# Two transformer blocks on one core: the third mixer's low parts on VectorE, its units summed in one PSUM bank, its factors folded

## The chip, the core and the metric

The kernel runs on one core of a Trainium2 chip. The metric is the device time of one execution in microseconds. All names of engines are those of the profile: TensorE (PE, and PEld for its weight loads), VectorE (DVE), ScalarE (ACT), GpSimd (POOL) and SyncE (SP), whose queue issues nearly all transfers.

## What is computed

One sequence of 256 tokens with 1024 features passes a first block (a norm, a mixer of pooling, mLSTM and attention, a feed-forward part) and then a second block of two layers. Each layer is feed-forward, mixer, feed-forward, with a layer norm behind each. The mixer of the first layer is a sparse attention (the second mixer of the kernel), that of the second layer is HGRN2, the third mixer, which the change is about:

```python
h = (x @ w_in).astype(F32)                      # 1024 x 4096
zq, zf, zi, zg = jnp.split(h, 4, axis=-1)       # 8 heads of 128 each
q = jax.nn.silu(zq)
log_f = jnp.logaddexp(jnp.log(lbf), jnp.log1p(-lbf) + jax.nn.log_sigmoid(zf))
k = (1.0 - lbf) * jax.nn.sigmoid(-zf)
# per head: S_t = f_t * S_(t-1) + k_t v_t,  o_t = q_t S_t   (v = zi)
o = o * lax.rsqrt(jnp.mean(o * o, axis=-1, keepdims=True) + RMS_EPS) * norm_gain
o = o * jax.nn.silu(zg)
return o.reshape(B, T, D_MODEL) @ w_out
```

`lbf` are bounds per feature, made by a softmax over the layers from a small input; `norm_gain` has one value for each of a head's 128 features. Inputs and output are float32.

## The kernel before, in words

**Products.** All large products are made from two parts of each operand: a high part (a copy to fp32r, on ScalarE, line 265 for weights) and a low part (the value minus the high part, line 268, on VectorE or on GpSimd). A product is hi x hi + hi x lo + lo x hi. Weights come in units of 1 MB, split in two halves of 128 x 1024 each; `get()` hands out the next half, loads units three ahead and splits five halves ahead. A half in the set `pool_halves` has its low part made by GpSimd; `on_pool(len(units) - 14)` puts there 28 halves of the third mixer's input weights, all but those of its first two units.

**Tokens and features.** Activations lie transposed in `XT`, eight chunks of 128 features, high and low part side by side. `gA` makes a unit with features on the partitions: of each half, a whole PSUM bank receives hi x (hi, lo) as one product of 512 columns and lo x hi as one of 256, eight times, so that two halves of the bank have to be added. `evA` does that, per half unit: ScalarE copies one half out (line 428, tile `evs`) and VectorE adds (line 429, tile `z`). `gB` makes a unit with tokens on the partitions, in two banks, one for each 128 tokens, by products of 256 columns. The banks of both come from a pool of two (`psa`).

**The third mixer** (`hgrn_mix`). It begins with the bounds `lb` and `om` = 1 - `lb`: eight small VectorE operations and one exponential (lines 1270 to 1283), and a load of the gain to all partitions. `bulk(u)` makes the four units of the heads 2u and 2u+1: zf, from which two sigmoids give `ff` and `kk` (lines 1312 and 1313), scaled by `om` and `lb` on VectorE (1316 and 1317); zq, which gives `qq` = sigmoid(zq) x zq (1320 and 1321); and the gate and the values (`gv`), with the gate multiplied by the gain on GpSimd (1302). `heads(u)` is the recurrence of two heads in seven levels: in each, TensorE multiplies `kk` with `qe` (lines 1353 and 1356), and VectorE then updates `qe` (1359), `kk` (1360) and `tot` (1362) in place and copies the products to `AT` (1370, or 1368 on ScalarE). After the levels come the products with the values, a norm whose power -1/2 is GpSimd's (516 and 518), and the turn into `MT` by TensorE transposes (`to_XT`, line 500), with a split behind them (487 and 490).

**Order.** `bulk(0)` runs alone; then `drive` lets one step of `bulk(u + 1)` (a half unit) alternate with one step of `heads(u)`, for u = 0, 1, 2, here called stages one, two and three. The last two heads run beside the first products of the output weights (`Out.early`), whose halves are split on VectorE. Instructions keep the order of their engine's queue at run time; where a step is traced is not fixed to the order of the code alone, since a scheduler places instructions by priority.

The first mixer's mLSTM (`mlstm`) makes its weights by eight exponentials at line 801 and multiplies them by products at line 812. `all_vecs` loads small vectors in SP's queue at the kernel's start, ahead of the third load of weights.

Of the kernel before, what the change touches and what calls it, by code (L numbers as in the profile page):

```python
# [9 lines left out]
F32 = mybir.dt.float32  # L10
F32R = mybir.dt.float32r
U32 = mybir.dt.uint32
AF = mybir.ActivationFunctionType
# [4 lines left out]
P = 128  # L18
# [18 lines left out]
# ---------------------------------------------------------------- constants of the shapes  # L37
# [17 lines left out]
def _make_constants():  # L55
# [20 lines left out]
    # rows 0-31: the bucket of the distance 255 - j; row 32: its mask  # L76
# [18 lines left out]
# ---------------------------------------------------------------- kernel  # L95
# [9 lines left out]
def _kern(ctx, tc, nc, A, out):  # L105
# [11 lines left out]
    # ---- x first, then the constants  # L117
    def new_x(rms=False):
        """a tile of tokens; rms: its last element makes the sum of the squares / D the mean of the squares + 1e-6"""
        t = xp.tile([P, D + 1], F32, tag="x", bufs=3, name=nm("x"))  # L120
        if rms:
            POOL.memset(t[:, D : D + 1], 32.0 * 1e-6 ** 0.5)
        return t
# [19 lines left out]
    def queue_behind(i, other):  # L143
        """i after the other in the order of their engine"""
# [3 lines left out]
    # ------------------------------------------------------------ weights  # L148
# [46 lines left out]
    for li in range(2):  # L195
# [14 lines left out]
        else:  # L210
# [4 lines left out]
            on_pool(len(units) - 14)  # L215
# [4 lines left out]
    PF = 3  # units loaded ahead  # L220
    ahead = [5]  # halves split ahead
    barrier = []  # VectorE's instruction that the next low parts wait for
    nxt = [0]  # the next half
    hold = [None, 0]  # the pool and the number of the halves that a feed-forward part holds to its end
# [63 lines left out]
    # ------------------------------------------------------------ small operands  # L288
# [19 lines left out]
    def all_vecs():  # L308
# [6 lines left out]
                ("lb", A["hgrn_lb_2"].rearrange("i (c p) -> (i c) p", p=P)),  # L315
            ]
# [9 lines left out]
    # ------------------------------------------------------------ matmul helpers  # L326
# [12 lines left out]
    later = []  # what is issued behind bulk products of so many ns, and the ns left  # L339

    def behind(ns, ins):
        """issues these, which are last in a chain of other engines, behind the bulk products that run beside that chain"""
        later.append([ns, ins])

    @contextmanager
    def after_bulk(ns):
        """TensorE's part of what is traced here"""
# [18 lines left out]
    def run(g):  # L366
        """the whole of a generator, and what it returns"""
# [6 lines left out]
    def drive(bulk, chains, n):  # L374
        """a step of bulk, then n steps of the chains, until bulk is done"""
# [10 lines left out]
    def gA(XT, alloc=None):  # L386
        """out[c, tok] of one unit of 256 columns, two banks [tt, (hi x hi, with a low part), 128]"""
# [10 lines left out]

    def mmA(XT, alloc=None):
        return run(gA(XT, alloc))  # L400

    def mmB_first(XT):
        """out[tok, c] of two units, the first 128 tokens before the others"""
# [31 lines left out]
    def gB(XT):  # L435
        """out[tok, c] of one unit: two banks, one of each 128 tokens"""
# [14 lines left out]
    def mmN(XT, n, pool, tag, bufs=1):  # L451
        """out[tok, (tt, c)] of a narrow unit of n columns"""
# [16 lines left out]
    def mmD(acc, H, k, w, tts, first, last, hfs=(0, 1)):  # L469
        """acc[tt][hf] += H[:, k] x one row chunk"""  # L470
# [21 lines left out]
    def split_T(XT, k, z):  # L492
        """both parts of z [P, 256 tokens] to chunk k"""
        split_to(XT[:, k, :, 0, :], XT[:, k, :, 1, :], z.rearrange("p (t c) -> p t c", t=2))

    def to_XT(XT, tt, x, k0=0, nk=8, ns=0):
        for q in range(0, nk, 4):
# [6 lines left out]
            split_to(XT[:, ks, tt, 0, :], XT[:, ks, tt, 1, :], ps[:, : w * P].rearrange("p (a b) -> p a b", a=w))  # L504
# [3 lines left out]
    # the table of the first functions  # L508
    ACT.activation(cp.tile([P, 1], F32, name="warm"), mhalf[:, 0:1], AF.Square)

    def rsqrt(src, n, eps):
        """(src + eps) ** -0.5, [P, n]; src in SBUF"""
# [29 lines left out]
    def ln_tile(tt, x, acc, gb, XT, final=False, ns=0):  # L542
# [6 lines left out]
        # mean / 32 and the mean  # L549
        V.tensor_scalar(st[:, 2:3], st[:, 0:1], st[:, 1:2], 1.0 / (32 * D), ALU.add, ALU.mult)  # L550
        # the last element makes the sum of the squares the variance + 1e-5
# [25 lines left out]
    # ------------------------------------------------------------ feed-forward  # L577
    def ffn(XT, conv, half, finish):
        with tc.tile_pool(name=nm("ff"), bufs=2) as fp:
# [17 lines left out]
            def turn(src):  # L597
                """[tok, tt, c] to a bank [c, tok]"""
# [964 lines left out]
```

## Time and profile before

| | us |
|---|---|
| time, median of 3 runs | 1442.87 |
| time, lowest and highest | 1440.56, 1442.90 |
| profiled execution, span from the first to the last instruction | 1438.1 |
| TensorE busy in that span | 1379.6 (96%) |
| VectorE busy | 992.7 (69%) |
| ScalarE busy | 735.8 (51%) |
| GpSimd busy | 189.1 (13%) |

Of the profiled execution the profile gives the span; its own time outside the span is not recorded, and the median stands 4.8 us above it. Matmuls are pipelined, so that a busy TensorE may still run at half its clock: the granted clock (PEclk, 1.00 is 2.4 GHz and 0.50 is 1.2 GHz) has to be read beside the busy time.

In rows that begin with two times and a colon, one stretch of the span is shown: its length, then busy time and number of instructions of TensorE, its weight loads, VectorE, ScalarE and GpSimd, the granted clock, the share of the DMA engines and GB/s. A row of one engine alone has that engine's busy time only. A timeline row has start and length in us, engine, line, operation, output and inputs, shapes and count, and in brackets the idle time before it and what ended it. A row of grouped instructions has, behind the bar, busy time in us and the mean ns of one, then the idle time before them and its releasers.

### The profile page before, as it was taken

Reading aid. Unit: us, or ns where it says so; the run is one execution under the profiler, and the core shown is the slowest. Engines: PE = TensorE matmul, PEld = TensorE weight load, DVE = VectorE, ACT = ScalarE, POOL = GpSimd, SP = SyncE. Lnnn points to the kernel's source line nnn. Section 1 sums busy time; section 2 is a strip of 40 time slices with the busy share of each in tenths; the row PEclk is TensorE's granted clock in tenths of the full one; section 3 lists DMA queues with packets and bytes.
Section 4 is the critical chain, followed back from the end, with each engine's and each line's share of the span. In section 5 each row is a group of like instructions: output and inputs, shape, how many; then the busy total and the mean of one; then the engine's idle time right before and its main releaser. Section 6 shows DMA issues by size and latency. Waiting matters only on the chain.

```text
span 1438.1 us, 20557 instructions
## 1 busy us (share of the span) xinstructions
PE 1379.6 (96%) x7993; PEld 1194.2 (83%) x7993; DVE 992.7 (69%) x1647; ACT 735.8 (51%) x1227; POOL 189.1 (13%) x127
## 2 busy tenths in 40 slices
PE   7899999999999999899999999999997999999997
PEld 6787888888888888688888888888886888788886
DVE  5865799986566766686765576566756777865574
ACT  5555554544554645576554463555643433654561
POOL 1220132120000005300000000000036560100000
PEclk9999999999999999799999999999998999999999
DMA  8433766555565766321665573555744333466560
GB/s 256 153 118 117 235 220 209 187 176 175 181 199 177 243 179 181 111 94 49 216 201 178 195 260 131 192 188 185 247 133 147 108 100 116 148 203 198 182 205 30
DMA packets 185567, 245.37 MB, mean 171 GB/s; under 512 B 7423, under 2 KB 164903, under 8 KB 185469
## 3 DMA queue, kind: packets, MB, share of 16 engines
q1 hardware_dynamic: 184653, 240.80, 51.4%
q0 software_dynamic: 816, 3.25, 0.7%
q8 instruction: 63, 1.03, 0.3%
q14 instruction: 35, 0.29, 0.1%
HBM read 242.95 MB, written 4.23 MB: 172 GB/s over the span
## 4 chain that ended last, share of the span: by engine, by line
PE 52%; DVE 4%; ACT 1%; POOL 1%; issue 1%; DVEq 0%; POOLq 0%; ACTq 0%
PE psa L355 21%; PE acc L355 14%; PE psb L355 12%; PE psb L1216 1%; PE psb L500 1%; PE lev L1356 1%; DVE kk L1360 1%; PE psb L1218 0%; DVE qe L1359 0%; PE psT L1199 0%; DVE ff L1316 0%; POOL rsr L518 0%; PE psS L1170 0%; DVE kk L1317 0%; PE lev L1353 0%
## 5 line engine op out<-in xcount | busy, mean ns | idle before, releaser
L265 ACT ACTIVATE hi<-raw 128x1024 fp32r<-128x1024 f32 x428 | 448.4, 1055 | 344.0 <-PE psa L355 148.4
L268 DVE TENSOR_TENSOR lo<-raw,hi 128x1024 fp32r<-128x1024 f32 x370 | 457.4, 1241 | 240.7 <-ACT hi L265 239.6
L355 PE MATMUL psa<-XT,hi 128*128 128x512 f32 x1136 | 413.4, 402 | 8.2 <-DVE z L429 8.1
L355 PE MATMUL psa<-XT,lo 128*128 128x256 f32 x1136 | 323.3, 285 | 0.0
L355 PE MATMUL psb<-XT,hi 128*128 128x512 f32 x800 | 282.3, 393 | 0.9 <-DVE z L429 0.9
L355 PE MATMUL acc<-hi,H 128*128 128x512 f32 x880 | 281.8, 393 | 0.0
L355 PEld LDWEIGHTS psa<-XT,hi 128*128 128x128 f32 x1136 | 216.7, 191 | 59.4 <-DVE z L429 9.3
L355 PE MATMUL psb<-XT,lo 128*128 128x256 f32 x800 | 223.6, 280 | 0.0
L355 PEld LDWEIGHTS psa<-XT,lo 128*128 128x128 f32 x1136 | 216.9, 191 | 3.6 <-issue 1.5
L355 PE MATMUL psa<-hi,XT 128*128 128x256 f32 (+1 forms) x928 | 200.4, 306 | 1.6 <-ACT XT L487 0.8
L268 POOL TENSOR_TENSOR lo<-raw,hi 128x1024 fp32r<-128x1024 f32 x58 | 148.1, 2566 | 398.0 <-ACT hi L265 360.4
L355 PEld LDWEIGHTS acc<-hi,H 128*128 128x128 f32 x880 | 166.0, 189 | 35.2 <-DVE H L490 0.3
L355 PEld LDWEIGHTS psb<-XT,hi 128*128 128x128 f32 x800 | 150.0, 187 | 36.7 <-DVE z L429 1.3
L355 PE MATMUL acc<-lo,H 128*128 128x512 f32 x440 | 173.7, 395 | 3.9 <-DVE lo L268 3.9
L355 PEld LDWEIGHTS psa<-hi,XT 128*128 128x128 f32 x928 | 153.0, 195 | 7.4 <-ACT XT L487 2.1
L355 PEld LDWEIGHTS psb<-XT,lo 128*128 128x128 f32 x800 | 150.1, 188 | 0.0
L355 PE MATMUL psa<-lo,XT 128*128 128x256 f32 (+1 forms) x464 | 131.7, 301 | 0.2 <-DVE lo L268 0.2
L355 PEld LDWEIGHTS acc<-lo,H 128*128 128x128 f32 x440 | 83.2, 189 | 21.3 <-DVE lo L268 4.8
L355 PEld LDWEIGHTS psa<-lo,XT 128*128 128x128 f32 x464 | 90.2, 194 | 2.4 <-DVE lo L268 0.5
L518 POOL TENSOR_TENSOR rsr<-var,mhalf 128x1 f32<-128x1 f32 x12 | 7.8, 647 | 626.9 <-ACT jk L556 626.9
L429 DVE TENSOR_TENSOR z<-psa,evs 128x256 f32<-128x256 f32 x132 | 55.1, 419 | 23.7 <-ACT evs L428 23.6
L428 ACT ACTIVATE evs<-psa 128x256 f32<-128x256 f32 x134 | 49.3, 368 | 19.2 <-PE psa L355 19.2
(351 smaller groups left out, 1335.3 us busy)
## 6 DMA issues: line engine op xcount, KB each, us to landing
raw<-in_ffn_w_gate_dram SPq DMA_DIRECT2D x44, 1024.0 KB, 5.1
raw<-in_ffn_w_up_dram SPq DMA_DIRECT2D x44, 1024.0 KB, 5.2
raw<-in_ffn_w_down_dram SPq DMA_DIRECT2D x44, 1024.0 KB, 5.0
raw<-in_w_up_dram SPq DMA_DIRECT2D x22, 1024.0 KB, 5.1
raw<-in_hgrn_w_in_dram SPq DMA_DIRECT2D x16, 1024.0 KB, 5.4
raw<-in_w_down_dram SPq DMA_DIRECT2D x11, 1024.0 KB, 4.8
raw<-in_nsa_w_in_dram SPq DMA_DIRECT2D x10, 1024.0 KB, 6.6
raw<-in_w_in_dram SPq DMA_DIRECT2D x9, 1024.0 KB, 6.5
```

What stands on the lines that cost most here:

```text
L265: h = ACT.activation(hi, src, AF.Copy)
L268: i = (POOL if j in pool_halves else V).tensor_tensor(lo, src, hi.bitcast(F32), ALU.subtract)
L355: i = PE.matmul(o, l, r, start=start, stop=stop)
L428: ACT.activation(s, p4[:, :, 1, :], AF.Copy)
L429: V.tensor_tensor(zc, p4[:, :, 0, :], s, ALU.add)
L500: ts = [PE.transpose(ps[:, j * P : (j + 1) * P], x[:, (q + j) * P : (q + j + 1) * P], ident) for j in range(w)]
L518: POOL.tensor_tensor(r[:, :n], src, mhalf[:, :n], ALU.pow)
L1216: PE.matmul(po5[:, 1, j % 2, br], T1[:, 2 * br + sb], vv[br][:, sb, vs], start=(sb == 0), stop=(sb == 1))
L1356: PE.matmul(pl[:, o : o + 64], kk[:, c, tt * P : (tt + 1) * P], q5[:, c, tt * nb : (tt + 1) * nb, 1, :], start=True, stop=True)
L1360: V.tensor_tensor(k5[:, :, :, 0, :], k5[:, :, :, 0, :], t4[:, :, :, 1, None].broadcast_to([P, 2, 2 * nb, m]), ALU.mult)
```

## The change

- The third mixer's 28 halves are no longer put in `pool_halves`; their low parts are made by VectorE.
- `gZ` takes the place of `gA` and `evA` for zf and zq: three products of 256 columns per chunk, all summed in one place, both half units in one bank. The sigmoids and the multiplication with zq read that bank.
- `kk` is no longer multiplied by `om`; `qq` is. `ff` is scaled on ScalarE. The gain is applied in `to_XT`, per partition, in the copy and in the split behind the transposes, and comes in with the small vectors.
- The bounds are made in the first mixer, on tiles that are kept, behind the exponentials of line 801.

Comments are left out in the changed file as well; those lines are not shown.

```diff
             for j in range(4):
                 for part in (1, 0, 3, 2) if j else (3, 2, 1, 0):
                     a_units(W, 1024 * part + 256 * j, 1, "A" if part < 2 else "B")
-            on_pool(len(units) - 14)
             b_units(A["hgrn_w_out_2"], [0, 1, 2, 3])
...
                 ("lb", A["hgrn_lb_2"].rearrange("i (c p) -> (i c) p", p=P)),
+                ("hg", A["hgrn_norm_gain_2"]),
...
+    def gZ(XT, alloc=None):
+        ps = (alloc or psa)()
+        for c in range(2):
+            hi, lo = get()
+            o = ps[:, 256 * c : 256 * c + 256].rearrange("p (t c) -> p t c", t=2)
+            for k in range(8):
+                bulk_mm(o, lo[:, k, :], XT[:, k, :, 0, :], k == 0, False)
+                bulk_mm(o, hi[:, k, :], XT[:, k, :, 0, :], False, False)
+                bulk_mm(o, hi[:, k, :], XT[:, k, :, 1, :], False, k == 7)
+            yield
+        return ps.rearrange("p (c t) -> p c t", c=2)
...
-    def to_XT(XT, tt, x, k0=0, nk=8, ns=0):
+    def to_XT(XT, tt, x, k0=0, nk=8, ns=0, gain=None):
...
-            split_to(XT[:, ks, tt, 0, :], XT[:, ks, tt, 1, :], ps[:, : w * P].rearrange("p (a b) -> p a b", a=w))
+            src = ps[:, : w * P].rearrange("p (a b) -> p a b", a=w)
+            if gain is None:
+                split_to(XT[:, ks, tt, 0, :], XT[:, ks, tt, 1, :], src)
+            else:
+                ACT.activation(XT[:, ks, tt, 0, :], src, AF.Copy, scale=gain)
+                V.scalar_tensor_tensor(XT[:, ks, tt, 1, :], src, gain, XT[:, ks, tt, 0, :].bitcast(F32), ALU.mult, ALU.subtract)
...
-                        ACT.activation(DT[:, h, tt, :], DT[:, h, tt, :], AF.Exp, bias=ee[:, tt, h : h + 1])
+                        i = ACT.activation(DT[:, h, tt, :], DT[:, h, tt, :], AF.Exp, bias=ee[:, tt, h : h + 1])
+                lower_bounds(mp, i)
...
+    bounds = [cp.tile([P, 8], F32, name=n) for n in ("lb", "om")]
+
+    def lower_bounds(mp, behind_):
...
+        V.tensor_tensor(lm, lbv[:, 0], lbv[:, 1], ALU.max)
+        V.tensor_tensor(e, lbv, lm[:, None, :].broadcast_to([P, 2, 8]), ALU.subtract)
+        queue_behind(ACT.activation(e, e, AF.Exp).ins, behind_)
+        V.tensor_tensor(lm, e[:, 0], e[:, 1], ALU.add)
...
-            hg = row_bc(A["hgrn_norm_gain_2"], 128, "hg", pool=mp)
+            lb, om = bounds
...
-                g3 = gz.rearrange("p t c d -> p (t c) d")
-                POOL.tensor_tensor(g3, g3, hg[:, None, :].broadcast_to([P, 4, P]), ALU.mult)
...
-                zf = evA(mp, (yield from gA(XT)), tag="zf", bufs=1)
+                zf = yield from gZ(XT)
...
                     h = 2 * u + c
-                    V.tensor_scalar(ff[:, c], ff[:, c], om[:, h : h + 1], lb[:, h : h + 1], ALU.mult, ALU.add)
-                    V.tensor_scalar(kk[:, c], kk[:, c], om[:, h : h + 1], None, ALU.mult)
-                zq = evA(mp, (yield from gA(XT)), tag="zq", bufs=1)
+                    ACT.activation(ff[:, c], ff[:, c], AF.Identity, scale=om[:, h : h + 1], bias=lb[:, h : h + 1])
+                zq = yield from gZ(XT)
...
                 ACT.activation(qq, zq, AF.Sigmoid)
-                V.tensor_tensor(qq, qq, zq, ALU.mult)
+                for c in range(2):
+                    h = 2 * u + c
+                    V.scalar_tensor_tensor(qq[:, c], qq[:, c], om[:, h : h + 1], zq[:, c], ALU.mult, ALU.mult)
...
-                    to_XT(MT, tt, oo[:, tt], 2 * u, 2, ns=HNS[tt] if u < 3 else 0)
+                    to_XT(MT, tt, oo[:, tt], 2 * u, 2, ns=HNS[tt] if u < 3 else 0, gain=vecs["hg"])
```

## Rows read from the trace of the kernel before

**Rows 1.** Busy time by stretch of the third mixer: two in the hole, three stages.
```profile
1088.30:1095.90 7.60, 0.03 (x2) 0.01 (x1) 7.57 (x7) 1.33 (x2) 6.40 (x3) 0.71 0.68 218
1095.90:1102.20 6.30, 6.30 (x21) 5.39 (x22) 2.49 (x8) 1.57 (x2) 0.00 (x0) 0.54 0.53 165
1102.20:1139.30 37.10, 33.83 (x250) 31.04 (x250) 28.28 (x41) 15.10 (x32) 22.93 (x13) 0.95 0.31 96
1139.30:1177.30 38.00, 34.72 (x254) 31.62 (x254) 29.46 (x45) 15.84 (x34) 22.98 (x14) 0.96 0.35 112
1177.30:1208.10 30.80, 29.83 (x233) 27.25 (x233) 24.62 (x48) 13.41 (x25) 6.41 (x4) 1.00 0.36 124
```

**Rows 2.** Timeline, 1077 to 1112 us: the first hole and an evacuation before it.
```profile
1080.86 0.36 ACT L428 ACTIVATE evs<-psa 128x256 f32<-128x256 f32 x1
...
1082.87 11.83 POOL L268 TENSOR_TENSOR lo<-raw,hi 128x1024 fp32r<-128x1024 f32 x5
...
1085.19 4.96 DVE L1316 TENSOR_SCALAR ff<-ff,om,lb 128x256 f32<-128x256 f32 x2 [0.70 <-ACT ff L1312]
...
1095.89 0.80 PE L355 MATMUL psa<-XT,hi 128*128 128x512 f32 x1 [7.57 <-DVE z L429]
```

**Rows 3.** VectorE's groups by shape in stage three, 1185.8 to 1213 us.
```profile
L268 DVE TENSOR_TENSOR lo<-raw,hi 128x1024 fp32r<-128x1024 f32 x6 | 7.4, 1226 | 2.0 <-ACT hi L265 2.0
...
L1359 DVE TENSOR_TENSOR qe<-qe,tot 128x256 f32<-128x256 f32 x6 | 2.5, 421 | 0.9 <-PE lev L1356 0.9
...
L429 DVE TENSOR_TENSOR z<-psa,evs 128x256 f32<-128x256 f32 x3 | 1.3, 424 | 0.0
...
L1316 DVE TENSOR_SCALAR ff<-ff,om,lb 128x256 f32<-128x256 f32 x2 | 0.7, 413 | 0.7 <-ACT ff L1312 0.7
```

**Rows 4.** Timeline, the holes of stage one (two rows) and of stage two.
```profile
1115.12 2.56 DVE L1359 TENSOR_TENSOR qe<-qe,tot 128x256 f32<-128x256 f32 x1
...
1118.16 0.63 PE L1356 MATMUL lev<-qe,kk 128*128 128x64 f32 x4 [2.69 <-DVE kk L1360]
...
1156.20 0.94 PE L1356 MATMUL lev<-qe,kk 128*128 128x64 f32 x4 [2.68 <-DVE kk L1360]
```

**Rows 5.** TensorE and its clock by stretch, behind the hole of stage one.
```profile
1118.20:1122.30 4.10, 4.10 (x21) 0.58 0.82 256
```

**Rows 6.** GpSimd's low parts of the mixer: shortest, median, longest ns.
```profile
L268 POOL TENSOR_TENSOR lo<-raw,hi x28: 2382/2412/2672, 1045.7 to 1182.4; 128x1024 fp32r<-128x1024 f32 x28
```

**Rows 7.** Busy time by stretch, the second half of stage three.
```profile
1191.00:1208.10 17.10, 17.10 (x152) 16.26 (x152) 14.21 (x29) 7.25 (x13) 1.28 (x1) 1.00 0.36 124
```

**Rows 8.** The chain that ended last: products of a feed-forward unit, and of values.
```profile
1007.49 5.64 PE psa L355 x32
...
1194.68 2.91 PE psa L355 x24
```

**Rows 9.** Groups by shape, 1040 to 1195 us: readers of PSUM, and GpSimd's powers.
```profile
L428 ACT ACTIVATE evs<-psa 128x256 f32<-128x256 f32 x17 | 6.2, 367 | 0.0
...
L518 POOL TENSOR_TENSOR rsr<-rsv,mhalf 128x2 f32<-128x2 f32 x4 | 2.9, 716 | 0.3
...
L1299 DVE TENSOR_TENSOR gz<-gz,psa 128x256 f32<-128x256 f32 x6 | 2.5, 414 | 4.6 <-ACT gz L1298 4.6
...
L487 ACT ACTIVATE XT<-psb 128x512 fp32r<-128x512 f32 x4 | 2.4, 598 | 6.1 <-PE psb L500 6.1
```

**Rows 10.** Timeline, the bounds at the mixer's start and TensorE's wait there.
```profile
1065.32 1.28 ACT L1274 ACT_TABLE_LOAD   x1 [3.08 <-DVE r L552]
...
1067.91 0.17 DVE L1282 TENSOR_SCALAR om<-lb 128x8 f32<-128x8 f32 x1
...
1069.52 0.63 PE L500 MATMUL psb<-ident,x 128*128 128x128 f32 x4 [0.50 <-DVE x L563]
```

**Rows 11.** Timeline of SP's queue: the last small vector, the third weight load.
```profile
10.60 0.32 SPq L297 DMA_DIRECT2D vst<-in_hgrn_lb_dram  x1
11.91 0.40 SPq L239 DMA_DIRECT2D raw<-in_w_in_dram  x1
```

More of the change, by code (lines that the diff above doesn't have):

```diff
@@ L1263, in nsa_mix @@
                     end(g)
+    bounds = [cp.tile([P, 8], F32, name=n) for n in ("lb", "om")]
+    def lower_bounds(mp, behind_):
+        lbv = vecs["lb"].rearrange("p (i h) -> p i h", i=2)
+        lb, om = bounds
+        lm = mp.tile([P, 8], F32, name="lm")
+        e = mp.tile([P, 2, 8], F32, name="lbe")
+        V.tensor_tensor(lm, lbv[:, 0], lbv[:, 1], ALU.max)
+        V.tensor_tensor(e, lbv, lm[:, None, :].broadcast_to([P, 2, 8]), ALU.subtract)
+        queue_behind(ACT.activation(e, e, AF.Exp).ins, behind_)
+        V.tensor_tensor(lm, e[:, 0], e[:, 1], ALU.add)
+        V.reciprocal(lm, lm)
+        V.tensor_tensor(e, e, lm[:, None, :].broadcast_to([P, 2, 8]), ALU.mult)
+        V.tensor_tensor(lb, e[:, 0], e[:, 1], ALU.add)
+        V.tensor_tensor(lb, lb, e[:, 0], ALU.subtract)
+        V.tensor_scalar(om, lb, -1.0, 1.0, ALU.mult, ALU.add)
     def hgrn_mix(XT, MT, W):
@@ L1268, in hgrn_mix @@
             load_consts(4, mp)
-            lbv = vecs["lb"].rearrange("p (i h) -> p i h", i=2)
-            lm = mp.tile([P, 8], F32, name="lm")
-            e = mp.tile([P, 2, 8], F32, name="lbe")
-            V.tensor_tensor(lm, lbv[:, 0], lbv[:, 1], ALU.max)
-            V.tensor_tensor(e, lbv, lm[:, None, :].broadcast_to([P, 2, 8]), ALU.subtract)
-            ACT.activation(e, e, AF.Exp)
-            V.tensor_tensor(lm, e[:, 0], e[:, 1], ALU.add)
-            V.reciprocal(lm, lm)
-            V.tensor_tensor(e, e, lm[:, None, :].broadcast_to([P, 2, 8]), ALU.mult)
-            lb = mp.tile([P, 8], F32, name="lb")
-            V.tensor_tensor(lb, e[:, 0], e[:, 1], ALU.add)
-            V.tensor_tensor(lb, lb, e[:, 0], ALU.subtract)
-            om = mp.tile([P, 8], F32, name="om")
-            V.tensor_scalar(om, lb, -1.0, 1.0, ALU.mult, ALU.add)
-            hg = row_bc(A["hgrn_norm_gain_2"], 128, "hg", pool=mp)
+            lb, om = bounds
             ATs = []
```

## The prediction

> **What bounds the kernel now.** I read the page's slices first: TensorE's row is full almost everywhere, so time can only come out of its few weak slices, and two of those lie where GpSimd's row is highest, in the third mixer. I then cut that mixer into stretches [rows 1]: a first hole at 1088 us, then three stages, in each of which the level chain of two heads runs beside the products of the next two. TensorE is busy 33.83 of 37.1 us in stage one and 34.72 of 38.0 in stage two, but 29.83 of 30.8 in stage three, in which GpSimd has 6.41 us left to do against 22.9. The granted clock has a mean of 0.71 and 0.54 in the two stretches from 1088.3 to 1102.2.
>
> The timeline of the first hole [rows 2] gives the reason. GpSimd subtracts low parts without a pause (11.83 us for five). Beside it two VectorE scalings of ff take 4.96 us; with GpSimd quiet one takes 413 ns [rows 3]. Two scalings of kk wait in the same way, and behind them in VectorE's queue stands the addition z (L429), which frees a PSUM bank: TensorE waits 7.57 us for it. In stage one a multiplication qe takes 2.56 us beside GpSimd [rows 4] (421 ns otherwise [rows 3]), and the products of the next level wait 2.69 us; stage two repeats this with 2.68 us. After each hole TensorE runs for a while at the lower of its two levels, 1.2 GHz: 4.1 us with a mean of 0.58 in stage one [rows 5]. Stage two has the same pattern (mean clock of the whole stage 0.96, stage one 0.95 [rows 1]).
>
> **The change part by part.** *Low parts move from GpSimd to VectorE.* 28 subtractions of 2.41 us leave GpSimd [rows 6]; one takes 1.226 us on VectorE [rows 3], 34.3 us more there in all, about 8 in each of stages one and two, the rest before and in the first stage. What leaves the path: the hole of 7.6 us, and 6.3 us at 0.54, worth 6.3 x 0.46 = 2.9: 10.5 us. Stage one: 2.7 us of waiting and 4.1 x 0.42 = 1.7 of clock: 4.4 us. Stage two the same, 4.4 us. Together 19.3 us.
>
> What is late next is VectorE's own load. Stage three is a model of it, since its splits (of the output weights) already run there: VectorE is busy 24.62 of 30.8 us [rows 1], and TensorE had no idle time in its last 17.1 us [rows 7], and 1.0 us in the whole. For a changed stage I take 24.62, minus four z of 0.42 and four scalings of about 0.41 [rows 3], plus two more splits (2.45): 23.8 us of some 32. That leaves a quarter of the stage free, so I charge stages one and two 0.7 us each, somewhat under stage three's idle time: 1.4 us. Bounds: 0, and the present hole come back, 4.4 us per stage.
>
> *Units summed in one bank.* Each of 16 half units was 8 products of 512 columns and 8 of 256; it becomes 24 of 256, the same columns. Two half units (32 products) of the first form take 5.64 us in the chain, so 2.82 each; 24 products of 256 columns of another unit take 2.91 [rows 8]. That costs 16 x 0.09 = 1.4 us, all on the path. The 16 evacuations on ScalarE (0.37 us) and 16 additions z on VectorE (0.42) vanish; they lay beside other work, apart from the hole counted above.
>
> A bank now holds a whole unit until its last reader is done. For zf these are two sigmoids on ScalarE, with the whole next unit as cover. For zq they are a sigmoid and two multiplications on VectorE: the nearest rows that read PSUM are 0.60 and 0.41 us [rows 9], so about 0.60 + 2 x 0.41 + 0.2 for two hand-overs = 1.6 us after the last product; before it was one evacuation and one addition, 0.8. Three times (heads 2 to 7) this bank is wanted after 12 products of the next unit, half of 2.91, and mostly the products of a level besides. With a high part ahead on ScalarE and a split ahead on VectorE, at 1.23 us for either, the hold is 4.1 us, 2.6 more than the 12 products. I take 0.4 us each, 1.2 in all, nearer to the case without a queue (0.15 each), since both engines are free for much of the stage; bounds 0 and 3 x 2.6 = 7.8. Below nothing it can come out as well: the path from zf to the sigmoids is shorter by 0.8 us, three times, 2.4 us.
>
> Now ScalarE empties the first half's bank at 1080.86 us [rows 2], while the second half is summed in another. The Trainium skill (PSUM — Partial Sum Buffer, PSUM bank collisions raise a hardware error) says that two engines have to be kept apart by bank, not by address. By it no reader of the first half starts before the unit's last product; if it could, this term would be 0.4 us in all and the sum 0.8 lower. No run here shows which.
>
> *Factors folded.* kk's scaling goes into qq, as a factor of its multiplication with zq. ff's goes to ScalarE: 8 instructions there against 16 evacuations removed. The gain leaves GpSimd for the splits behind the transposes, which keep their number: a scaled copy on ScalarE, and on VectorE a form with one operand more. I take 0; the cover is the quarter of the stage in which VectorE is free, and without it I would put 0.1 us on each of 16, 1.6 us.
>
> *Bounds.* A table load (1.28 us) and an exponential leave ScalarE from their place ahead of a layer norm's square, and eight VectorE operations of some 0.17 us go with them [rows 10]. The square then begins 1.3 us earlier; the transposes at the end of its chain found TensorE idle for 0.50 us. Gain 0.5, not more, since before that hole TensorE has other products. In the first mixer the same work comes behind the last exponential of the mLSTM weights (L801), with the table already loaded. There VectorE's sum of the exponentials waits for ScalarE, and behind it would stand the product at L812, which the mLSTM's values need; TensorE has bulk products meanwhile. I take 0.5 us; bounds: 0, and 8 x 0.17 plus a wait as long as a high part and the exponential, some 3 us. A small transfer more in SP's queue puts the third weight load later by at most 1.3 us [rows 11]; the products of the first two units hide that, and without them it costs as much.
>
> **Sum.** Gains 19.3 + 0.5 = 19.8; costs 1.4 + 1.4 + 1.2 + 0.5 = 4.5. Net 15.3 us against the profiled span of 1438.1: 1422.8. The median of the times, 1442.87, lies 4.8 us above that span; with the same distance the forecast is 1427.6.
>
> **The rivals.** *A smaller gain: new holes.* VectorE serves level chain, splits and banks in order; where these meet, TensorE idles long enough to lose its clock. Price: the 4.4 us of stage one in each of three stages, 13.2 us in place of the 2.6 charged for load and banks: 1438. For it: qq's two readings hold a whole bank. Against it: 17.1 us without idle time beside splits on VectorE [rows 7].
>
> *Slower: splits wait at the head of VectorE's queue.* A split needs its high part from ScalarE; issued too early it stops VectorE. The six of stage three waited 2.0 us together [rows 3]; if each waited as long as that, 8 add 16 us per stage to 23.8 us of work and to the 8.8 us that VectorE stands now (37.1 - 28.28 [rows 1]): 48.6 us, 11 more than the present 37.6, in each of two stages. Against that stand 11 us gained in the first hole and the bounds: 11 us slower, 1454. It decides once VectorE's waits in a stage pass 37.6 + 5.5 - 23.8 = 19 us. Against it: 8.8 us now, and 2.0 for six splits.
>
> *The rest of GpSimd still blocks.* Eight powers for rsqrt stay there, 0.72 us each [rows 9], and a split beside one would stop as qe does now [rows 4]: 5.8 us if felt each time, 1433. The Trainium skill (SBUF — State Buffer, Who interferes with whom) has it that VectorE with two SBUF inputs and GpSimd reading SBUF shut each other out for a whole instruction; the trace agrees, with 2.56 us against 0.42. Against the price: VectorE mostly waits for just these powers.
>
> *It does not do what it says:* the holes have a cause other than GpSimd, and only the costs are left: 1447. Against it: the same scaling takes six times as long beside GpSimd as without it.
>
> **How the numbers follow.** Forecast 1427.6, chance 0.69, its own range 1422 (load, bank and first mixer at nothing, zf's 2.4 us gained) to 1432. New holes 0.13, GpSimd's rest 0.10, slower 0.05, another cause 0.03. The range for 8 in 10 reaches from 1420 to 1437. A measurement of this kernel tells 0.2% (2.9 us) from no change. Faster by more: 0.69 + 0.10 + 0.10 = 0.89; slower 0.05 + 0.02 = 0.07; within it the rest, 0.04.
>
> **What would show it.** After: no hole near 1088 us, the clock at 1.00 through the mixer, stages of 31 to 33 us, VectorE's two-input operations at 0.42 us throughout, half units at 2.9. Wrong would be: TensorE idle above 1 us for qq or for a low part, VectorE standing for high parts, a longer mLSTM part in the first mixer.

## The result, and the profile after

The changed kernel takes 1420.87 us (median of 4 runs, 1419.54 to 1423.34), the kernel before 1442.88 beside it (4 runs, 1440.56 to 1444.89): a ratio of 0.9852, with a 95% interval of 0.9838 to 0.9866. That is 22.0 us, where 15.3 were forecast; the time lies inside the range and 6.7 us under the forecast. The profiled span went from 1438.1 to 1417.7 us, 20.4 less, so 5.1 us of the 6.7 are in the span. The other 1.6 us lie in the distance of the median from the profiled span, 4.8 us before and 3.2 now; the forecast had carried the 4.8 over. The changed kernel's profiled execution took 1419.54 us, 1.8 us above its own span, so the rest of the 3.2 is only that this execution was faster than the median.

The page shows it at a glance, in 40 equal slices of the span, each digit a share in tenths. First TensorE and GpSimd in the kernel before, then TensorE, GpSimd and the clock in the changed one:

```profile
PE   7899999999999999899999999999997999999997
...
POOL 1220132120000005300000000000036560100000
```

```profile
PE   7899999998999999799999999999999999999997
...
POOL 1320221220000003500000000000000000100000
PEclk9999999999999999899999999999999999999999
```

The third mixer lies in slices 31 to 35 of the changed kernel. TensorE's row has only nines there, and GpSimd's only zeros up to a 1 in the last; before, the 31st slice of TensorE was a 7. TensorE's two weak slices behind the start are now the 10th and the 17th; the latter, where GpSimd's row has its 5 and the clock its only 8, comes back below.

Busy time by stretch, the changed kernel: the stretch from the mixer's start to the first level, then stages one, two and three (columns as in rows 1):

```profile
1063.60:1090.30 26.70, 26.70 (x227) 26.70 (x226) 18.10 (x31) 15.57 (x22) 1.53 (x3) 1.00 0.50 164
1090.30:1122.10 31.80, 31.80 (x281) 31.02 (x280) 21.16 (x41) 14.64 (x28) 0.27 (x2) 1.00 0.46 143
1122.10:1155.60 33.50, 32.90 (x287) 31.71 (x286) 22.62 (x46) 15.89 (x32) 1.93 (x5) 1.00 0.38 127
1155.60:1186.40 30.80, 30.21 (x261) 28.97 (x260) 22.27 (x45) 14.35 (x25) 1.54 (x3) 1.00 0.37 129
```

Against [rows 1] stage one went from 37.1 to 31.8 us, stage two from 38.0 to 33.5, stage three stayed at 30.8. The stretch ahead of them took 38.0 before (1064.18 to 1102.18) and takes 26.7 (1063.64 to 1090.31). The granted clock is 1.00 throughout, where it was 0.71 and 0.54 in the hole and 0.95 and 0.96 in the stages. That is where the time went: 11.3 + 5.3 + 4.5 = 21.1 us, all inside the third mixer. Its whole length, from the last product ahead of it to the transposes of its last output tile, went from 170.7 to 149.7.

What TensorE waited for from 1060 to 1215 us, the changed kernel (engine, line, waited for: us in total, times, longest):

```profile
PE psb L513 <- DVE oo L1419: 1.9, 7, 0.3
```

This is the whole list. Before, from 1060 to 1240 us, 8.3 us for z and 6.0 us for kk stood in it:

```profile
PE psa L355 <- DVE z L429: 8.3, 2, 7.6
PE lev L1356 <- DVE kk L1360: 6.0, 5, 2.7
```

And VectorE's groups in stage one (1090.3 to 1122.1 us), to be held against [rows 3, 4]:

```profile
L267 DVE TENSOR_TENSOR lo<-raw,hi 128x1024 fp32r<-128x1024 f32 x8 | 9.8, 1226 | 4.2 <-ACT hi L264 4.2
...
L1382 DVE TENSOR_TENSOR qe<-qe,tot 128x256 f32<-128x256 f32 x6 | 2.5, 422 | 1.8 <-PE lev L1379 1.8
L1383 DVE TENSOR_TENSOR kk<-kk,tot 128x256 f32<-128x256 f32 x6 | 2.5, 418 | 0.0
...
L1344 DVE SCALAR_TENSOR_TENSOR qq<-qq,om,psa 128x256 f32<-128x256 f32 x2 | 0.9, 472 | 0.0
```

qe takes 422 ns in the mean instead of up to 2.56 us, and the eight splits of the stage cost VectorE 1226 ns each, with 4.2 us of standing for high parts in all.

### The profile page after: what moved, and what is told of

It reads as the page before. It is cut to its first block, busy times and chain, and to the rows that moved or that the text cites. A ratio compares the mean times of both kernels' runs of the same rounds, so it can differ in the third digit from the quotient of the medians.

```text
span 1417.7 us, 20750 instructions
## 1 busy us (share of the span) xinstructions
PE 1373.5 (97%) x8121; PEld 1194.8 (84%) x8121; DVE 971.8 (69%) x1647; ACT 734.9 (52%) x1218; POOL 116.6 (8%) x95
## 4 chain that ended last, share of the span: by engine, by line
PE 50%; issue 6%; DVE 1%; ACT 1%; POOL 1%; DVEq 0%; POOLq 0%; ACTq 0%
PE psa L355 19%; PE acc L355 13%; PE psb L355 12%; PE psb L1235 1%; PE psb L513 1%; PE psb L1237 0%; POOL rsr L536 0%; PE psT L1218 0%; PE psS L1189 0%; PE lev L1379 0%; PE psT L1220 0%; PE psb L1180 0%; PE psS L1147 0%; PE psS L1191 0%; ACT hi L264 0%
## 5 line engine op out<-in xcount | busy, mean ns | idle before, releaser
L267 DVE TENSOR_TENSOR lo<-raw,hi 128x1024 fp32r<-128x1024 f32 x398 | 492.5, 1243 | 252.2 <-ACT hi L264 251.1
L355 PE MATMUL psa<-XT,hi 128*128 128x512 f32 (+1 forms) x1264 | 410.9, 375 | 3.2 <-DVE z L442 3.0
L355 PEld LDWEIGHTS psa<-XT,hi 128*128 128x128 f32 x1264 | 230.3, 189 | 48.5 <-DVE z L442 4.2
L355 PE MATMUL psa<-hi,XT 128*128 128x256 f32 (+1 forms) x928 | 197.4, 302 | 0.4 <-ACT XT L500 0.3
L355 PEld LDWEIGHTS psa<-hi,XT 128*128 128x128 f32 x928 | 150.8, 192 | 6.2 <-ACT XT L500 1.9
L267 POOL TENSOR_TENSOR lo<-raw,hi 128x1024 fp32r<-128x1024 f32 x30 | 81.1, 2715 | 192.1 <-ACT hi L264 167.4
L442 DVE TENSOR_TENSOR z<-psa,evs 128x256 f32<-128x256 f32 x116 | 48.3, 418 | 16.2 <-ACT evs L441 15.9
L500 ACT ACTIVATE H<-sg 128x512 fp32r<-128x512 f32 x51 | 31.7, 622 | 48.4 <-DVE sg L626 33.8
```

What stands on the lines that cost most here:

```text
L267: i = (POOL if j in pool_halves else V).tensor_tensor(lo, src, hi.bitcast(F32), ALU.subtract)
L355: i = PE.matmul(o, l, r, start=start, stop=stop)
L442: V.tensor_tensor(zc, p4[:, :, 0, :], s, ALU.add)
L500: i = ACT.activation(hi, src, AF.Copy)
```

## The experiments

The theory (A): GpSimd's subtractions stretch VectorE's operations, and their departure from the third mixer is the gain; folding, one bank and bounds only move some us. The rival (B): the shorter chain on VectorE, with its z additions and scalings gone, is a good part of the gain by itself. Each ratio below is to the kernel before, run beside that experiment, with a 95% interval; the length of the mixer is that of one profiled execution.

**The one line alone.** The kernel before, without its subtractions on GpSimd in the third mixer; the rest of the change is left out.

```diff
-            on_pool(len(units) - 14)
             b_units(A["hgrn_w_out_2"], [0, 1, 2, 3])
```

> The kernel before with one line taken out: the 28 low parts of the third mixer are made by VectorE; units are still summed in two halves, factors and bounds stay where they were. Theory A (GpSimd's subtractions are the cause of the holes, the rest is worth nothing): nearly the whole gain, 1421 to 1425 us. Theory B (the holes need both, GpSimd's work and the operations that the folding takes away): VectorE carries more here than in the changed kernel, so new holes, 1430 us or more.

Measured: 1423.41 us (1420.73 to 1424.55), ratio 0.9875 (0.9858 to 0.9892). The mixer is 150.8 us long. One deleted line gives nearly the whole gain: 19.9 of the mixer's 21.0 us, and by the two ratios 18 of 21 us. What TensorE still waited for, 1060 to 1218 us:

```profile
PE lev L1355 <- DVE kk L1359: 1.9, 2, 0.9
PE psb L499 <- DVE oo L1395: 0.7, 3, 0.3
PE psa L354 <- DVE z L428: 0.7, 1, 0.7
PE psb L499 <- DVE x L562: 0.5, 1, 0.5
```

The list still names z and kk, as before the change, but for 2.6 us in place of 14.3. The last line is the layer norm's wait at the mixer's start, which stood there before the change as well [rows 10].

**All but the one line.** The changed kernel, with the subtractions back on GpSimd in that mixer.

```diff
+            on_pool(len(units) - 14)
             b_units(A["hgrn_w_out_2"], [0, 1, 2, 3])
```

> The changed kernel with that one line put back: GpSimd makes the 28 low parts, all else as changed. Theory A: GpSimd still blocks VectorE's operations with two SBUF inputs, and the loss is nearly whole, 1437 to 1442 us. Theory B (two ways to cure the first hole, each enough): the scalings and the additions behind which TensorE stood in the first hole are gone, so only the holes of stages one and two return, 4.4 us each, 1429 to 1432 us.

Measured: 1442.5 us (10 runs, 1436.75 to 1445.21), ratio 1.0003 (0.9989 to 1.0017); the mixer is 168.9 us long. B falls: with GpSimd subtracting, the folded form is worth nothing that the times tell, and 1.8 us by the length of the mixer. TensorE's three longest waits, 1060 to 1230 us, below them two of VectorE's groups from 1080 to 1180, and two rows of VectorE's timeline in the hole:

```profile
PE psS L1360 <- DVE qq L1345: 5.3, 1, 5.3
PE lev L1380 <- DVE kk L1384: 4.5, 4, 1.3
PE lev L1377 <- DVE kk L1384: 3.3, 2, 1.7
```

```profile
L1384 DVE TENSOR_TENSOR kk<-kk,tot 128x256 f32<-128x256 f32 x12 | 13.7, 1142 | 0.0
...
L1345 DVE SCALAR_TENSOR_TENSOR qq<-qq,om,psa 128x256 f32<-128x256 f32 x6 | 2.6, 471 | 0.0
```

```profile
1087.23 9.66 DVE L1386 TENSOR_TENSOR tot<-tot 128x128 f32<-128x128 f32 x6
1096.81 0.86 DVE L1345 SCALAR_TENSOR_TENSOR qq<-qq,om,psa 128x256 f32<-128x256 f32 x2
```

The hole is there although z is gone: it now waits for qq. And qq itself takes 471 ns, no more than in the changed kernel (472). What holds it up stands ahead of it in VectorE's queue: seven small products of the factors (tot), on two operands in SBUF, which took 1.64 us (the first) and 9.66 us (the other six) here. Operations on two SBUF operands are stretched (kk 1142 ns in the mean against 418); the one that reads one operand from SBUF and one from PSUM is not. Two operands are not the whole rule, though: in the first hole of the kernel before, the stretched ones were scalings of ff, with a single tensor in SBUF beside their factors (2.48 us each [rows 2]); with the line deleted the same eight scalings take 412 ns in the mean.

**Reading or presence?** Two kernels keep VectorE's splits as in the change and give GpSimd other work beside them. In the first, GpSimd subtracts a high part from itself, into a tile that nothing uses, at each split of the mixer: work added for this run alone, which reads SBUF as the old subtractions did. In the second, GpSimd only writes: a memset of 128 x 2048, also unused, triggered by a one-column copy on ScalarE.

```diff
+        if j in beside and spare:
+            f = hi.rearrange("p a b -> p (a b)").bitcast(F32)
+            POOL.tensor_tensor(spare[0], f, f, ALU.subtract)
```

> The changed kernel, in which GpSimd makes a subtraction of the same size beside each split of those 28 halves that falls into the mixer (it reads the high part twice and writes a tile that nobody uses); VectorE still makes the low parts, so nothing waits for GpSimd but the buffer of the high part. Theory A (the port between them, not the result's lateness, is what costs): VectorE's two-input operations take up to 2.5 us again, holes and lower clock return, 8 to 25 us slower than the changed kernel. Rival (what cost was that the low parts came late): within 3 us of the changed kernel.

Measured: 1456.72 us (1452.37 to 1457.95), ratio 1.0101 (1.0078 to 1.0125); the mixer is 183.5 us long, 33.8 more than without the reads. That is beyond the 8 to 25 us expected: VectorE now makes its own low parts beside these reads, and they are stretched as well, to 1571 ns in the mean from 1226. TensorE's four longest waits, 1060 to 1240 us, and two of VectorE's groups from 1080 to 1200:

```profile
PE psS L1364 <- DVE qq L1349: 8.3, 1, 8.3
PE lev L1404 <- DVE kk L1388: 6.5, 2, 3.2
PE lev L1384 <- DVE kk L1388: 5.7, 4, 1.8
PE lev L1381 <- DVE kk L1388: 4.1, 4, 1.9
```

```profile
L268 DVE TENSOR_TENSOR lo<-raw,hi 128x1024 fp32r<-128x1024 f32 x24 | 37.5, 1571 | 10.4 <-ACT hi L265 10.4
L1388 DVE TENSOR_TENSOR kk<-kk,tot 128x256 f32<-128x256 f32 x12 | 15.1, 1262 | 0.0
```

```diff
+        if j in beside and spare:
+            queue_behind(ACT.activation(spare[1], spare[0][:, 0:1], AF.Copy).ins, h)
+            POOL.memset(spare[0], 0.0)
```

> The changed kernel with a fill of a 128x2048 tile by GpSimd (it writes and reads nothing) at each split of the 28 halves that falls into the mixer, started by a one-column copy on ScalarE. Theory A (GpSimd's reading is what shuts VectorE's second input out): VectorE's two-input operations keep 0.42 us and splits 1.23; only the 28 small copies on ScalarE cost, 0 to 4 us over the changed kernel. Rival (any work of GpSimd at VectorE's side blocks): like the run with GpSimd's subtractions beside the splits, 8 us slower or more.

Measured: 1420.76 us (1419.26 to 1422.08), ratio 0.985 (0.9828 to 0.9872): nothing lost, the mixer is 149.7 us long as without. GpSimd's group from 1060 to 1240 us, and two of VectorE's from 1070 to 1190:

```profile
L275 POOL MEMSET spare<- 128x2048 f32 x27 | 48.9, 1810 | 43.6 <-ACT mark L274 43.6
```

```profile
L268 DVE TENSOR_TENSOR lo<-raw,hi 128x1024 fp32r<-128x1024 f32 x32 | 39.0, 1226 | 14.7 <-ACT hi L265 14.5
...
L1390 DVE TENSOR_TENSOR kk<-kk,tot 128x256 f32<-128x256 f32 x18 | 7.5, 419 | 0.0
```

With 48.9 us of GpSimd beside it, kk stays at 419 ns and a split at 1226. So a busy GpSimd isn't what hurts, nor its writing of this kind: its reading is. An instruction of GpSimd with a single input wasn't tried. The Trainium skill (SBUF — State Buffer, Who interferes with whom) has it so, down to the case of writing alone: a VectorE instruction with two SBUF inputs and a GpSimd instruction that reads SBUF exclude each other, and one with at most one SBUF input isn't touched unless it runs in a mode that uses both of VectorE's ports. Both runs and qq's 471 ns agree. By that rule the scalings of ff would have run in such a mode; no run here shows it.

**Two banks for a unit.** The changed kernel, with zf and zq summed in halves, evacuated by ScalarE and added by VectorE as before; the scalings stay folded.

```diff
-                zf = yield from gZ(XT)
+                zf = evA(mp, (yield from gA(XT)), tag="zf", bufs=1)
...
-                zq = yield from gZ(XT)
+                zq = evA(mp, (yield from gA(XT)), tag="zq", bufs=1)
```

> The changed kernel with zf and zq made as before (two halves in two banks, an evacuation and an addition), all else as changed. By the working of the prediction the one bank costs 1.4 us of products and 1.2 us of waiting: 2.6 us faster than the changed kernel, 1418. Rival (the one bank is worth something, since 16 additions leave VectorE): 1 to 3 us slower, 1422 to 1424.

Measured: 1424.1 us (1421.25 to 1424.86), ratio 0.9879 (0.9863 to 0.9896); the mixer is 151.1 us long. One bank is not a cost but a gain of 1.4 us by the length of the mixer, which is 149.7 us in each of three profiled kernels with one bank (the changed one, the one with the writes and the one with the gain on GpSimd, below). The two ratios give 3.9 us (0.0027 of 1442), but their intervals overlap, so the times alone don't show the sign and the size is open. The sign by the profile is not what I forecast. The chain of waits, 1060 to 1110 us, shows why, first with two halves, then the changed kernel, and last two of TensorE's waits with two halves, 1060 to 1215 us:

```profile
1069.87 17.26 PE psa L355 x114
1087.15 0.56 DVE lo L267
1087.72 0.58 issue
1088.30 0.43 DVE z L442
...
1092.74 2.81 PE psa L355 x16
...
1096.39 2.87 PE psa L355 x16
```

```profile
1069.96 20.34 PE psa L355 x170
1090.31 0.89 PE psS L1359 x8
1091.19 2.88 PE psa L355 x24
...
1094.91 2.93 PE psa L355 x24
```

```profile
PE lev L1379 <- DVE kk L1383: 1.9, 2, 0.9
PE psa L355 <- DVE z L442: 1.7, 1, 1.7
```

In the two-halves form the addition z stands behind a split in VectorE's queue, and TensorE waits for the bank that z frees (1.7 us, its only wait of that kind). In one bank there is no z to stand anywhere. With two halves TensorE also waits 1.9 us for kk, and 1.2 us less than in the changed kernel for oo (0.7 against 1.9). The price per half unit is there, somewhat under the 0.09 us forecast: 2.88 and 2.93 us for 24 products against 2.81 and 2.87 for 16, about 1.0 us in 16. Together 1.7 + 1.9 - 1.2 - 1.0 is the 1.4 us of the mixer's length; why kk waits wasn't tried.

**Bounds and gain put back.** Two small parts, each undone alone in the changed kernel: the bounds made at the start of the third mixer again, and the gain multiplied in by GpSimd again.

```diff
-                lower_bounds(mp, i)
...
             load_consts(4, mp)
+            lower_bounds(mp, None)
             lb, om = bounds
```

> The changed kernel with the bounds made at the start of the third mixer again. By the prediction's working the move gains 0.5 us at the third mixer and costs 0.5 in the first: no difference, within 1.5 us of the changed kernel. Rival (the table load and the eight operations were worth their whole length): 2 us slower or more.

Measured: 1422.99 us (1422.07 to 1423.19), ratio 0.9859 (0.9842 to 0.9876).

```diff
+                g3 = gz.rearrange("p t c d -> p (t c) d")
+                POOL.tensor_tensor(g3, g3, hg[:, None, :].broadcast_to([P, 4, P]), ALU.mult)
...
-                    to_XT(MT, tt, oo[:, tt], 2 * u, 2, ns=HNS[tt] if u < 3 else 0, gain=vecs["hg"])
+                    to_XT(MT, tt, oo[:, tt], 2 * u, 2, ns=HNS[tt] if u < 3 else 0)
```

> The changed kernel with the gain multiplied on GpSimd again, four times 1.29 us with two inputs read. By the prediction's working the folding is worth nothing: within 1.5 us. By the port's exclusion each of the four can stop VectorE for up to 1.29 us: 0 to 5 us slower, with two-input operations of VectorE above 0.42 us beside them.

Measured: 1422.07 us (1420.89 to 1422.66), ratio 0.9853 (0.9832 to 0.9874). Neither can be told from the changed kernel. With the bounds back the mixer is 150.4 us long, 0.6 more, near the 0.5 forecast; with the gain back it is 149.7, the same. The four multiplications by GpSimd do stop VectorE, as the expectation had it. One product of the factors takes 980 ns in the mean beside them (1070 to 1190 us); in the changed kernel it takes 174:

```profile
L1388 DVE TENSOR_TENSOR tot<-tot 128x16 f32<-128x16 f32 x4 | 3.9, 980 | 0.1
```

But TensorE's waits in the mixer are the same as in the changed kernel. So not every such instruction costs time: it has to meet a chain that TensorE waits for.

**The same elsewhere.** If reading by GpSimd is the cause, the 30 low parts that GpSimd still makes in the changed kernel should cost something too: 4 in the first mixer (the expectation below says five), 12 in the second, 14 in the first block's feed-forward part. Three kernels take them away: those of the first mixer, those of the second, and all 30.

```diff
-    pool_halves.update(FP)
```

> The changed kernel with the first mixer's five GpSimd low parts moved to VectorE as well. Theory A carried over: the hole of 3.0 us before an addition z at about 62 us goes, and part of the 12 us at half clock behind it: 4 to 8 us faster than the changed kernel. Rival: VectorE is full there (3.9 of 4 us in most stretches from 32 to 52 us), so five splits of 1.23 us land on the path and eat the gain: within 2 us, or slower.

```diff
-            on_pool(len(units) - 9)
```

> The changed kernel with the second mixer's GpSimd low parts (twelve, 2.4 us each) moved to VectorE. Theory A carried over: four two-input operations for KL, 8.73 us beside GpSimd, take 2.8 us; TensorE's wait of 6.3 us for vblk and 2.2 for QS go, and most of the time at half clock between 580 and 600 us (mean 0.75): 9 to 13 us faster. Rival (VectorE becomes late with splits there, 12 x 1.23 us): under 4 us faster.

```diff
-    pool_halves.update(FP)
...
-    pool_halves.update(range(2 * n0 + CF[0], 2 * len(units) - 6, CF[1]))
-    pool_halves.update(2 * len(units) + h for h in CP)
...
-            on_pool(len(units) - 9)
```

> The changed kernel with no low part on GpSimd anywhere: 30 more go to VectorE, of which about 13 in the first feed-forward part. Theory A: the gains of the first and second mixer add up, 12 to 20 us faster than the changed kernel. Rival: in the first feed-forward part, whose convolution fills VectorE, the splits are late and cost 3 us or more, so less than the run with the second mixer alone.

Measured: 1414.2 us (1413.9 to 1416.4), ratio 0.9808 (0.9786 to 0.983); 1414.47 (1412.09 to 1414.91), 0.9803 (0.9781 to 0.9826); 1407.44 (1404.28 to 1412.16), 0.9763 (0.9728 to 0.9797). Beside the kernel with the memsets on the same chip, which has the time of the changed one, that is 6.6, 6.3 and 13.3 us less. In the first mixer the wait of 3.0 us for z is gone, and the gain lies in the range of 4 to 8 us expected. The expectation of 9 to 13 us for the second mixer was too high. Its place is the 17th slice of the page, the weak one. The timeline there, VectorE, first in the changed kernel, then with the splits of the second mixer on VectorE:

```profile
572.19 8.73 DVE L1113 TENSOR_TENSOR KL<-z,KH 64x512 fp32r<-64x512 f32 x4 [1.03 <-ACT KH L1112]
```

```profile
574.89 2.78 DVE L1112 TENSOR_TENSOR KL<-z,KH 64x512 fp32r<-64x512 f32 x4
```

Four subtractions KL take 8.73 us beside GpSimd and 2.78 without it. In the changed kernel TensorE waits behind them, and its clock falls (waits from 560 to 600 us, and the stretch from 580 to 600):

```profile
PE psT L1097 <- DVE vblk L1100: 6.3, 1, 6.3
```

```profile
580.00:600.00 20.00, 16.24 (x74) 13.97 (x75) 11.29 (x37) 7.16 (x17) 7.80 (x4) 0.75 0.39 145
```

Without GpSimd the wait is gone and the clock is 1.00 in that stretch. The wait and 20 x 0.25 us of clock would make 11 us; smaller waits came in their place (0.8 to 1.4 us each, for mx, nr and z), and 6.3 is left.

Last, the first and second mixer both, with the feed-forward's 14 low parts left to GpSimd:

```diff
-    pool_halves.update(FP)
...
-            on_pool(len(units) - 9)
```

> The changed kernel with the low parts of the first and the second mixer on VectorE, those of the first feed-forward part left on GpSimd. If the first feed-forward part is indifferent, the two single gains (6.5 and 6.5 us) add up, 1407 to 1409 us, the same as with no low part on GpSimd anywhere. If VectorE is full in that part, this is the fastest version, 1403 to 1405; if GpSimd disturbs there as well, 1411 to 1413.

Measured: 1406.35 us (1403.29 to 1409.68), ratio 0.9745 (0.9721 to 0.977). It has the lowest time of the study, 14.5 us under the changed kernel and 15.7 under the kernel with the gain on GpSimd, which ran on the same chip; the two single gains add up to 12.9 (6.6 + 6.3). Its interval overlaps that of the kernel without any low part on GpSimd, so in the sum the 14 in the feed-forward part cost nothing that the times tell. The traces show that this is a balance of two effects. With these low parts on GpSimd (the first two rows below, last kernel) an operation of the convolution takes 2.53 us where it otherwise takes 0.48, and TensorE waits 3.7 us for a low part further down VectorE's queue. With all of them on VectorE (the third row, the kernel without any on GpSimd) that wait is gone, and one of 4.4 us for z stands at another place in that part:

```profile
310.69 2.53 DVE L606 SCALAR_TENSOR_TENSOR cy<-z,vec,cy 128x255 f32<-128x255 f32 x1
...
322.00 0.50 PE L353 MATMUL acc<-lo,H 128*128 128x512 f32 x1 [3.69 <-DVE lo L265]
```

```profile
170.76 0.77 PE L351 MATMUL psa<-XT,hi 128*128 128x512 f32 x1 [4.41 <-DVE z L438]
```

## Why the prediction was right, and where it was off

**What bounded the kernel.** Right. The one line alone shortens the mixer by 19.9 us, and the rest without it by 1.8. The chain that [rows 2, 3] suggested (GpSimd reads, VectorE's two-operand instruction stretches, the bank or the level comes late, TensorE stands, its clock falls) holds at each link: 422 ns for qe, no wait for a bank or a level, clock 1.00. Two readings need a correction. The page before has one weak slice of TensorE in the third mixer, the 31st, and not two; the other, the 17th, lies in the second mixer, where GpSimd's row is high as well. And the scalings of ff in the first hole have only one tensor operand, so that they are not two-input operations in the sense of qe or kk.

**Low parts: gross gain.** In the first stretch 10.5 us of hole and clock, 0.5 for the bounds and four half units at 0.09 make 10.6; it gained 11.3. Stages one and two were put at 4.4 each from one named wait and the clock behind it. That was too narrow, and [rows 1] already had the rest: in stage one 37.1 - 33.83 = 3.3 us without TensorE and 37.1 x 0.05 = 1.9 of clock make 5.1; in stage two 3.3 + 38.0 x 0.04 = 4.8. After the change no idle time is left in stage one and 0.6 in stage two. Less 0.4 for four half units that gives 4.7 and 3.8; measured are 5.3 and 4.5.

**VectorE's load: 1.4 us charged, none seen.** VectorE is busy 21.16 us of 31.8 and 22.62 of 33.5, below the 23.8 of some 32 that I had from stage three, and no wait of TensorE leads to a split. This is the first mis-sized term.

**One bank: 2.6 us charged, 1.4 us gained by the mixer's length.** The second mis-sized term, and its sign was wrong. Its part for the longer half units (1.4) was nearly right, with about 1.0. Its part for zq's bank (1.2) was not felt: in stage one the sigmoid begins at 1101.64 and the two multiplications end at 1104.35, and TensorE meanwhile has the products of two levels and 12 products into the other bank. What I had left out of the balance was z's place in the queue. I had called z hidden apart from the hole already counted; with splits on VectorE it would have stood behind one of them again, as the two-halves kernel shows. So taking z away kept the moved splits from making a new hole of 1.7 us. The 2.4 us that I named as possible through the earlier sigmoids aren't told apart from this.

The sigmoids, the first readers of zf and zq, take a whole unit in one instruction (128x512), so nothing here could have read the first half early, and no run shows what the rule of the Trainium skill on readers of a bank (PSUM — Partial Sum Buffer, PSUM bank collisions raise a hardware error) would have cost.

**Factors folded: nothing charged.** Right in the sum. ff's scaling on ScalarE takes 600 ns for 128x256, more than the evacuation it replaces (367 ns [rows 9]); ScalarE is busy 14.64 of 31.8 us in stage one and hides it. Only the gain was undone alone; the two scalings weren't.

**Bounds.** The 0.5 us in the third mixer agree with the 0.6 by which it is longer when they are put back. The 0.5 us in the first mixer can't be told: it ends at 132.53 us in the changed kernel and at 132.91 with the bounds out of it, but from 132.2 to 135.4 in the profiled kernels that have the same code up to there. All of these end later than the kernel before (129.54) and the one with the line alone (130.93). VectorE's first operation of the first norm already starts at 8.86 us instead of 7.41, and the third weight load is issued at 14.07 instead of 11.91, 2.2 us later where I allowed at most 1.3 [rows 11]. The added transfer itself explains 1.3 of it; 0.9 stand ahead of it in SP's queue, behind the first weight loads, and no kernel was made that tells why. In the profiled execution the changed kernel reaches the third mixer 0.5 us ahead again, but that may be luck: the six profiled kernels with the same code up to that mixer reach it between 1063.5 and 1068.4 us, the two with the old code at 1064.2 and 1065.0. So it stays open whether the late start costs something in the sum; on the average of these it would be about 1 us.

**After the mixer** 1.1 us were lost again, most of it behind the layer norm's hole, which the prediction hadn't foreseen. It can't be put down to the change: the clock fell there in three of thirteen profiled kernels, one of them with GpSimd's subtractions back (last section).

**Together.** By stretch: 11.3 + 5.3 + 4.5 + 0.0 for stage three, less 0.2 in the tail, is 20.9 against 15.8 forecast for the mixer; 0.5 ahead of it and -1.1 behind it make the span's 20.4 to within rounding. Of the 5.1 us above the forecast, stages one and two give 2.4 and 1.6, stage three 0.8 and the first stretch 0.7, and the tail takes its 0.2 back (the rest is rounding). The time came 1.6 us nearer to the span than forecast, which is the choice of the profiled execution and no merit of the change.

**The rivals.** New holes of 4.4 us: none, though the 1.7 us with two banks were their beginning. Splits that wait at the head of VectorE's queue: 4.2 us of standing for eight in stage one, far from the 16 at which that rival was priced. The rest of GpSimd: the powers for rsqrt are still there, and oo, which comes behind them, is all that TensorE still waits for in the mixer: 1.9 us, seven times at most 0.3 each; before it was 1.3. Another cause: excluded by the first two experiments and by the one with reads.

## What to carry to other kernels

Before work is moved to an idle GpSimd to relieve a busy VectorE, look at what VectorE does beside it: where a latency chain there works on two SBUF operands, a GpSimd instruction that reads SBUF can hold that chain up by about its own length (qe took 2.56 us instead of 0.42 beside subtractions of 2.41), and the engine that looked relieved becomes the late one; the writes tried here were harmless, and so were four reads that met no chain that TensorE waits for. To price a removed wait, take the whole stage's idle time and clock, not the one wait that has a name. And when work is added to an in-order queue, ask which small instruction that frees a buffer will stand behind it: removing that instruction can be worth more than its 0.4 us.

## What the runs showed of the hardware that was not expected

Where GpSimd reads costs very unequally: 4 subtractions in the first mixer cost 6.6 us, 12 in the second 6.3, 28 in the third 18 to 20, and 14 in a feed-forward part nothing measurable, where the wait that goes without them (3.7 us) is replaced by another (4.4). The count says nothing; what stands beside it does.

The stretch is not only for large instructions. The six products of tot, from 128x128 down to 128x4, took 9.66 us together beside GpSimd; in the changed kernel's stage one those six take between 156 and 283 ns each.

The same hole doesn't always lower the clock. Behind the mixer TensorE waits for a layer norm, 2.00 us in the changed kernel and 1.99 before; the eight transposes that follow (timeline, the changed kernel first, then before) take 1.94 and 1.29 us:

```profile
1221.63 1.94 PE L513 MATMUL psb<-ident,x 128*128 128x128 f32 x8 [2.00 <-DVE x L581]
```

```profile
1243.06 1.29 PE L500 MATMUL psb<-ident,x 128*128 128x128 f32 x8 [1.99 <-DVE x L563]
```

The products behind them go on at 0.41 us where they took 0.28; the granted clock is 0.50 from 1221.6 to 1223.4 us, and 1.00 behind the hole of the kernel before. Of the thirteen profiled kernels two more show it, the one with the gain on GpSimd (1.88 us) and the one with GpSimd's subtractions back (1.75); in the other ten the eight transposes take 1.29 us behind a hole of 1.99 or 2.00. What decides it stays open.
